# Out-gate of a decoder layer by seven block products, low weight parts by adding transfers, second values moved into the heads

## The chip, the cores and the metric

The kernel runs on one core of one Trainium2 chip. The metric is the device time of one execution in microseconds; for one core that is the time of that core. The time before is the median of three runs.

## The reference, cut to what matters

One layer works on 512 tokens and 1024 channels, in float32. Only what the change touches is shown.

```python
u = _rmsnorm(h, norm1_g[l])
proj = u @ w_in[l]
a_glu, q, k, v, r, g_low, gate_a, gate_b = _split_cols(proj)   # 2048|512|512|1024|1024|16|1024|1024

c = a_glu[..., :CONV_CH] * jax.nn.sigmoid(a_glu[..., CONV_CH:])
c = _causal_dwconv(c, conv_dw_w[l], conv_dw_b[l])               # 31 taps for each channel
c = jax.nn.silu(_layernorm(c, conv_ln_g[l], conv_ln_b[l]))      # over channels
y_conv = c @ w_conv_out[l]

gk = jax.nn.log_sigmoid((g_low @ w_gate_up[l] + b_gate[l]).astype(jnp.float32)) / GATE_NORMALIZER
o = _gla_chunked(qh, kh, vh, gkh)                               # 4 heads, dk 128, dv 256
o = o * lax.rsqrt(jnp.mean(o * o, axis=-1, keepdims=True) + EPS) * gla_norm_g[l]
o = o.reshape(bsz, seq, GLA_VDIM).astype(x.dtype) * jax.nn.silu(r)
y_gla = o @ w_gla_out[l]

merged = jax.nn.sigmoid(gate_a) * y_conv + jax.nn.sigmoid(gate_b) * y_gla
h = h + merged @ w_o[l]
# then a channel mixer (up-projection, 3-tap convolution, silu gate, down-projection) and a norm
```

The out-gate is `r`: a product of the 512 x 1024 activations `u` with a 1024 x 1024 slice of `w_in`, whose silu multiplies the normed output of the heads.

## The kernel before, in words

**Products in three parts.** Every large product is made from a high and a low part of both operands. A weight block of 128 x 1024 is loaded by a transfer on SP's queue (L174, tile `raw`, four buffers), ScalarE rounds it to the high part (L254, `whi`), VectorE subtracts to get the low part (L257, `wlo`; four buffers each). `mm3` (L299 to L301) issues three TensorE matmuls of 128 x 128 by 128 x 512 for each piece of a product. `col_tile` makes one 128-channel tile of the result for all 512 tokens: eight pieces, 24 matmuls, out of one weight block. `row_half` makes results that are token-major (128 tokens by 512 channels).

**Order of weights.** The list `order` holds all weight blocks in the order of their use: `w_v` (first half), `w_glu` (two blocks for each of eight channel tiles, the gate block first), `w_low`, `w_v` (second half), for each of the four heads `w_qk` twice and `w_r` twice, then `w_gb` and `w_gla` in turns, `w_ga`, `w_conv`, `w_o`, and the channel mixer's. `weight(name, j)` hands out the next block and, before that, splits the blocks up to `LOOK = 2` ahead (`prefetch`, `split_weight`); each split issues one more load (`load`), so that loads are four blocks ahead.

**Product by seven.** `w_o` and `w_down` are multiplied by a scheme with seven instead of eight block products (names `a11`, `a12`, `s1`, `n2`, `s4`, `n3`, `a22` in `STEPS`). The weight sums that it needs are made by transfers on the GpSimd queue that add onto a block that lies in SBUF (`sum_on`, L225, and `load_block`, L208) and by VectorE (`operand`); their blocks are split at L238 and L239.

**Work between.** The convolution's 240 VectorE steps (L591), the layer norm's sums (L614), centring (L639 to L646) and output (`ln_out`, L658 to L669) stand in lists, `chains`. `fill(RATE)`, called by every `weight`, takes pieces with shares that add up to 5 and traces them behind the last low part (`pace`). What the source traces is put in each engine's queue by a scheduler, by its own estimate of when an instruction can run; `manual_schedule` keeps the source's order for the first part (up to the end of the first values) and for one group of ScalarE's.

**The start.** The four token tiles are transposed (L374), tokens 0 and 1 are multiplied first without their norm factor (L467), tokens 2 and 3 are normed before they are transposed and split by `spread_gain` in pieces of 128 x 128 (L384, L386). `renormed` (L479) makes the normed `u` for tokens 0 and 1 after that. The result stands in `u1` as high and low parts; whole float32 values aren't kept.

**The heads.** In round `h` of the loop over heads the decays (L760, L762), queries and keys of head `h` are made, and scores, states and outputs of head `h - 1`; between these stand two tiles of the out-gate (`gate_r`, channel-major, silu at L860). `outputs` takes the root of the mean square by GpSimd (`rsqrt`, L347), ScalarE scales (L843); `gated` transposes (L849), VectorE multiplies with the gain and the gate's tile (L852), and the result is split (L668, L669). In a fifth round `w_gb` tiles stand in the gaps.

Of the kernel before, what the change touches and what calls it, by code (L numbers as in the profile page):

```python
# [36 lines left out]
RATE = 5.0  # L37
WARM = 10
# [3 lines left out]
SEVEN = {"w_o": KT // 2, "w_down": FT // 2}  # L42
# [6 lines left out]

C_A, C_G, C_Q, C_K, C_V, C_R = 0, 1024, 2048, 2560, 3072, 4096  # L50
# [15 lines left out]
def trunk_layer(ctx: ExitStack, tc: tile.TileContext, a: dict, out: bass.AP):  # L66
# [20 lines left out]
    gla_scope, gp = scoped("gla", 1, "right")  # L87

# [92 lines left out]
    def block(name, pairs, d, row, col):  # L181

        pairs = pairs[2 * d : 2 * d + 2]
        first = pairs[0][row]
        w = a[name][col * SEVEN[name] + first // 2]
        return w if len(pairs) == 2 else w[:, row * T : (row + 1) * T]

    def keep_tile(name):
        if name == "w_o":
            return tp.tile([P, D], F32, tag="x", name=nm("kept"), bufs=3)  # L190
        return fp.tile([P, D], F32, tag="kept", name=nm("kept"), bufs=2)
# [21 lines left out]
    def operand(raw, pairs, step, d):  # L213

        if step == "s4":
            return kept[pairs, d, "b22"]
        if step == "n2":
            nc.vector.tensor_tensor(kept[pairs, d], kept[pairs, d], raw, ALU.add)
        return raw if step in ("a12", "n3") else kept[pairs, d]

    def sum_on(name, pairs, step, d):

        if step in ("a11", "n2"):
            nxt = block(name, pairs, d, *((0, 1) if step == "a11" else (1, 0)))
            nc.gpsimd.dma_start(kept[pairs, d], nxt, accum_op=ALU.add)  # L225

    def split_weight(between=None):
        if len(ready) < len(order):
            while len(raws) <= len(ready):
                load()  # L230
            raw = raws[len(ready)]
            name, spec = order[len(ready)]
            if name in SEVEN:
                raw = operand(raw, *spec)
# [4 lines left out]
                nc.vector.tensor_tensor(lo, raw, hi.bitcast(F32), ALU.subtract)  # L239
                sum_on(name, *spec)  # L240
                ready.append((hi, lo))
                load()
                return
            hi = wp.tile([P, D], F32R, tag="whi", name=nm("whi"), bufs=4)
            if order[len(ready)][0] == "w_low":
                nc.scalar.copy(hi, raw)
                if order[len(ready)][1] == 0:
                    part_lo = lambda t: t.rearrange("p (k c) -> p k c", c=P)[:, :, :RANK]
                    nc.vector.tensor_tensor(part_lo(hi), part_lo(raw), part_lo(hi.bitcast(F32)), ALU.subtract)
                ready.append((hi, None))  # L250
                load()
                return
            lo = wp.tile([P, D], F32R, tag="wlo", name=nm("wlo"), bufs=4)
            nc.scalar.copy(hi, raw)  # L254
            if between:
                between()
            pace[0] = nc.vector.tensor_tensor(lo, raw, hi.bitcast(F32), ALU.subtract)  # L257
            ready.append((hi, lo))
            load()
# [6 lines left out]
    def weight(name, j, ahead=LOOK):  # L266
        assert order[used[0]] == (name, j)
        prefetch(1)
        used[0] += 1
        prefetch(ahead)  # L270
        fill(RATE)
        return ready[used[0] - 1]
# [199 lines left out]

    def renormed(t):
        rb = ax_bank()[:, :P]
        nc.tensor.matmul(rb, r1[t].to_broadcast([P, P]), ident, start=True, stop=True)
        rb = rb.unsqueeze(1).to_broadcast([P, 4, P])
        for g in range(2):
            f = unscaled[t, g]
            nc.vector.tensor_tensor(by_token(f), by_token(f), rb, ALU.mult)  # L479
        for g in range(2):  # L480
            f = unscaled[t, g]
            split_by(by_token(f), *(u1[g][i][:, :, t * P : (t + 1) * P] for i in range(2)))
# [45 lines left out]
    here = lambda t: (lambda g, k: tuple(u1[g][i][:, k, t * P : (t + 1) * P] for i in range(2)))  # L528
# [24 lines left out]
    spread_gain(banks[2], 0, here(2))  # L553
# [5 lines left out]
    spread_gain(banks[3], 0, here(3))  # L559
# [13 lines left out]
    def values(n, middle):  # L573
        row_half("w_v", n * KT // 2, n, acts1, KT, v_done, n == 1, middle)

# [4 lines left out]

    conv = [None] * KT

# [9 lines left out]

    for k in range(KT):
# [6 lines left out]
        chains.append(  # L600
            [(1 if tap < CW - 1 else 0, lambda k=k, tap=tap, c=c: conv_tap(k, tap, c)) for tap in reversed(range(CW))]
        )


    ca = [None] * KT
    stat = {}

    def add_up(tiles, key):
        def first():
            stat[key] = btmp()  # L610
            nc.vector.tensor_tensor(stat[key], tiles(0), tiles(1), ALU.add)

        def more(k):
            nc.vector.tensor_tensor(stat[key], stat[key], tiles(k), ALU.add)  # L614

        return [first] + [lambda k=k: more(k) for k in range(2, KT)]
# [55 lines left out]
    def norm_chain():  # L672
        chain = [(1, f) for f in add_up(lambda k: conv[k], "sum")]
        chain[-1] = (RATE, chain[-1][1])
        chain.append((0, ln_mean))
        chain.extend((2, lambda k=k: ln_center(k)) for k in range(KT))
        chain[-1] = (RATE, chain[-1][1])
        chain.append((RATE, ln_var))
# [29 lines left out]
    def gate(step):  # L708
        if step > 0:
            return  # L710
        with tc.manual_schedule(engines={ET.Activation}):
            for h in range(HEADS):
                pg = ax_bank() if h < 3 else mm_bank()
                nc.tensor.matmul(pg, gate_up[:, h * DK : (h + 1) * DK], glow, start=True, stop=True)
                bg = pp[:, PP_BG + h : PP_BG + h + 1]
                ab.append(heap())
                nc.scalar.activation(ab[h], pg, AF.Abs, bias=bg)
                ls.append(heap())
                nc.vector.tensor_scalar(ls[h], pg, bg, 0.0, ALU.add, ALU.min)
            for h in range(HEADS):  # L720
                nc.scalar.activation(ab[h], ab[h], AF.Exp, scale=-1.0)
            for h in range(HEADS):
                nc.scalar.activation(ab[h], ab[h], AF.Ln, bias=1.0)
                nc.vector.tensor_tensor(ls[h], ls[h], ab[h], ALU.subtract)

    values(1, gate)


# [17 lines left out]
    class Head:  # L746
# [77 lines left out]
        def outputs(self):  # L824
            self.o = tp.tile([P, NT, DV], F32, tag="x", name=nm("o"), bufs=3)
            for g in range(2):
# [14 lines left out]
                for i in range(2):  # L841
                    o = self.o[:, 2 * g + i, :]
                    nc.scalar.activation(o, po[:, i * DV : (i + 1) * DV], AF.Copy, scale=r[:, i : i + 1])  # L843

        def gated(self):
            for s in range(2):
# [3 lines left out]
                f = tmp()  # L850
                m = 2 * self.h + s
# [3 lines left out]
    sr = [None] * KT  # L855

    def gate_r(m):
        pr = col_tile(weight("w_r", m), acts1)
        sr[m] = heap()
        nc.scalar.activation(sr[m], pr, AF.Silu)  # L860

    gbs = {}

    def gate_b(m):
        gbs[m] = col_tile(weight("w_gb", m), acts1)


    heads = [Head(h) for h in range(HEADS)]
    for h in range(HEADS + 1):
# [5 lines left out]
        else:  # L875
            gate_b(0)
        if old:
            old.scores()
        new.keys() if new else gate_b(1)
        if old:  # L880
            old.states()
        gate_r(2 * h) if new else gate_b(2)
        if old:
            old.outputs()
        gate_r(2 * h + 1) if new else gate_b(3)
# [6 lines left out]
    part = [None] * KT  # L892
    ma = [None] * KT
    for m in range(KT):
        part[m] = heap()
        nc.scalar.activation(part[m], gbs.pop(m), AF.Sigmoid)
        py = col_tile(weight("w_gla", m), oa)
        if m + AHEAD < KT:
            gate_b(m + AHEAD)
        nc.vector.tensor_tensor(part[m], py, part[m], ALU.mult)  # L900
    gas = {}
    for m in range(KT):
        pg = col_tile(weight("w_ga", m), acts1)
        gas[m] = heap()
        nc.scalar.activation(gas[m], pg, AF.Sigmoid)
    while chains:
        fill(1)
    H = T // 2
# [362 lines left out]
```

## Time and profile before

| what | value |
|---|---|
| median of 3 runs | 840.23 us (839.93 to 840.76) |
| the profiled execution's own time | 841.55 us |
| its span (first to last instruction) | 839.8 us |
| granted TensorE clock | 0.998 |
| TensorE busy (PE) | 829.0 us, 99% |
| VectorE busy (DVE) | 650.0 us, 77% |
| ScalarE busy (ACT) | 397.6 us, 47% |
| GpSimd busy (POOL) | 45.0 us, 5% |

The page lists busy times of the engines, the span in 40 slices, the transfer queues (q1 is SP's, q0 is GpSimd's), the chain of work that ended last, the costliest groups of instructions by line with the mean duration of one in ns, and the transfers with the time to landing. A matmul's duration overlaps with the next one's; what a matmul costs is the distance of two starts. All times in the text are in microseconds from the start of the span.

### The profile page before, as it was taken

The numbers are of one execution on the slowest core, as the hardware profiler recorded it, in microseconds if no ns is written. First come the engines' busy times: TensorE is split into PE (matmuls) and PEld (weight loads), VectorE is DVE, ScalarE is ACT, GpSimd is POOL, SyncE is SP. The second block draws the span as 40 slices with busy tenths as digits, with TensorE's granted clock in tenths as the row PEclk, the third lists the DMA queues.
The fourth block names the chain that finished last, engine by engine and source line by source line (L and its number), as shares of the span: only waits on it lengthen the run. The fifth ranks groups of instructions, "written<-read, shape, count | busy, mean of one in ns | idle before, by whom it ended". The sixth has DMA issues, their size and how long they took to land.

```text
span 839.8 us, 10108 instructions
## 1 busy us (share of the span) xinstructions
PE 829.0 (99%) x3841; PEld 692.3 (82%) x3841; DVE 650.0 (77%) x953; ACT 397.6 (47%) x590; POOL 45.0 (5%) x64
## 2 busy tenths in 40 slices
PE   8999999999999999999999999999999999999996
PEld 7888888887888888888888898888888888888885
DVE  5689879999997799644678758778757787677795
ACT  5722337435443422449444766444434444444454
POOL 1000000002100100000001000000100010000111
PEclk9999999999999999999999999999999999999999
DMA  7332222222222322222347643234742249222452
GB/s 289 119 105 101 96 96 91 91 87 80 97 76 76 125 89 89 100 81 95 101 100 197 180 151 126 101 94 108 213 150 87 66 89 284 102 84 94 102 124 100
DMA packets 28609, 97.27 MB, mean 116 GB/s; under 512 B 3248, under 2 KB 3648, under 8 KB 28560
## 3 DMA queue, kind: packets, MB, share of 16 engines
q1 hardware_dynamic: 25072, 84.82, 28.9%
q0 software_dynamic: 3456, 11.80, 8.0%
q8 instruction: 30, 0.49, 0.2%
q14 instruction: 19, 0.16, 0.1%
q10 hardware_dynamic: 32, 0.01, 0.0%
HBM read 94.51 MB, written 2.10 MB: 115 GB/s over the span
## 4 chain that ended last, share of the span: by engine, by line
PE 87%; DVE 9%; ACT 1%; issue 1%; POOL 1%; POOLq 0%; ACTq 0%; DVEq 0%
PE mm L299 26%; PE mm L301 26%; PE mm L300 26%; DVE c L591 4%; DVE wlo L257 2%; PE ax L301 1%; PE ax L300 1%; PE ax L299 1%; POOL rstd L347 1%; PE ax L832 1%; PE ax L374 1%; PE ax L434 1%; PE ax L814 0%; PE ax L834 0%; PE ax L849 0%
## 5 line engine op out<-in xcount | busy, mean ns | idle before, releaser
L299 PE MATMUL mm<-uh,wlo 128*128 128x512 f32 (+1 forms) x768 | 295.1, 384 | 0.0
L301 PE MATMUL mm<-uh,whi 128*128 128x512 f32 (+1 forms) x768 | 292.6, 381 | 0.0
L300 PE MATMUL mm<-ul,whi 128*128 128x512 f32 (+1 forms) x768 | 292.4, 381 | 0.0
L254 ACT CAST whi<-raw 128x1024 fp32r<-128x1024 f32 x116 | 120.9, 1048 | 128.5 <-PE mm L301 97.0
L257 DVE TENSOR_TENSOR wlo<-raw,whi 128x1024 fp32r<-128x1024 f32 x116 | 141.3, 1221 | 34.5 <-ACT whi L254 34.3
L301 PEld LDWEIGHTS mm<-uh,whi 128*128 128x128 f32 x768 | 144.5, 188 | 27.7
L300 PEld LDWEIGHTS mm<-ul,whi 128*128 128x128 f32 x768 | 144.7, 188 | 27.1
L299 PEld LDWEIGHTS mm<-uh,wlo 128*128 128x128 f32 x768 | 144.6, 188 | 26.8
L591 DVE SCALAR_TENSOR_TENSOR c<-h,pp,c 128x511 f32<-128x511 f32 (+14 forms) x240 | 162.7, 734 | 0.7
L1054 DVE SCALAR_TENSOR_TENSOR tmp<-mm,pp,tmp 128x511 f32<-128x511 f32 x88 | 65.8, 749 | 66.7 <-ACT tmp L1052 65.6
L1052 ACT ACTIVATE tmp<-mm,pp 128x512 f32<-128x512 f32 x44 | 34.3, 779 | 61.6 <-PE mm L301 61.6
L238 ACT CAST whi<-kept 128x1024 fp32r<-128x1024 f32 (+1 forms) x32 | 31.6, 994 | 23.7 <-PE mm L301 10.4
L239 DVE TENSOR_TENSOR wlo<-kept,whi 128x1024 fp32r<-128x1024 f32 (+1 forms) x32 | 36.7, 1154 | 4.2 <-ACT whi L238 4.1
L997 DVE TENSOR_TENSOR hres<-hres,mm 128x512 f32<-128x512 f32 (+1 forms) x49 | 32.7, 672 | 6.0 <-PE mm L301 4.1
L238 ACT CAST whi<-raw 128x1024 fp32r<-128x1024 f32 (+1 forms) x24 | 23.7, 995 | 17.9 <-PE mm L301 17.7
L347 POOL TENSOR_TENSOR rstd<-var,mhalf 128x1 f32<-128x1 f32 (+1 forms) x16 | 16.6, 1046 | 239.3 <-DVE var L839 194.8
L239 DVE TENSOR_TENSOR wlo<-raw,whi 128x1024 fp32r<-128x1024 f32 (+1 forms) x24 | 27.4, 1154 | 2.2 <-ACT whi L238 2.1
L300 PE MATMUL mm<-wlo,sh 128*128 128x512 f32 x66 | 25.8, 391 | 0.0
L301 PE MATMUL mm<-whi,sh 128*128 128x512 f32 x66 | 25.7, 390 | 0.0
L299 PE MATMUL mm<-whi,sl 128*128 128x512 f32 x66 | 25.6, 390 | 0.0
L299 PE MATMUL mm<-h,wlo 128*128 128x512 f32 x64 | 25.4, 398 | 0.0
L225 POOL DMA_DIRECT2D kept<-in_w_down_dram x12 | 10.4, 863 | 272.9 <-DVE wlo L239 272.9
(253 smaller groups left out, 1165.6 us busy)
## 6 DMA issues: line engine op xcount, KB each, us to landing
raw<-in_w_up_dram SPq DMA_DIRECT2D x44, 512.0 KB, 3.4
raw<-in_w_glu_dram SPq DMA_DIRECT2D x16, 512.0 KB, 3.5
raw<-in_w_down_dram SPq DMA_DIRECT2D x15, 512.0 KB, 3.3
kept<-in_w_down_dram POOLq DMA_DIRECT2D x10, 512.0 KB, 5.2
raw<-in_w_v_dram SPq DMA_DIRECT2D x8, 512.0 KB, 4.1
raw<-in_w_qk_dram SPq DMA_DIRECT2D x8, 512.0 KB, 3.2
raw<-in_w_r_dram SPq DMA_DIRECT2D x8, 512.0 KB, 3.2
raw<-in_w_gb_dram SPq DMA_DIRECT2D x8, 512.0 KB, 3.3
```

Of the source, the lines that this page charges most:

```text
L238: nc.scalar.copy(hi, raw)
L239: nc.vector.tensor_tensor(lo, raw, hi.bitcast(F32), ALU.subtract)
L254: nc.scalar.copy(hi, raw)
L257: pace[0] = nc.vector.tensor_tensor(lo, raw, hi.bitcast(F32), ALU.subtract)
L299: nc.tensor.matmul(acc, ll, rh, start=first, stop=False, **kw)
L300: nc.tensor.matmul(acc, lh, rl, start=False, stop=False, **kw)
L301: nc.tensor.matmul(acc, lh, rh, start=False, stop=last, **kw)
L347: nc.gpsimd.tensor_tensor(r, v, mhalf[:, :n], ALU.pow)
L591: nc.vector.scalar_tensor_tensor(y[:, s:], c[:, : T - s], w, y[:, s:], ALU.mult, ALU.add)
L997: nc.vector.tensor_tensor(hres[t, n][:, c], hres[t, n][:, c], bank[of[step]][i][:, c], op)
L1052: nc.scalar.activation(z, acc, AF.Identity, bias=pp[:, PP_FB + m : PP_FB + m + 1], scale=w[2])
L1054: nc.vector.scalar_tensor_tensor(z[:, s:], acc[:, : T - s], w[j], z[:, s:], ALU.mult, ALU.add)
```

## The change

Five things change together.

1. **The out-gate by seven.** `w_r` joins `SEVEN`. A new routine `unit` makes seven block products, token-major, into six accumulators, right after `w_low` and before the heads: 7 products x 2 token tiles x 4 pieces x 3 matmuls. `r_sink` adds them up in eight tiles `sr[t, n]` and takes the silu. The weight sums come from adding transfers; one more than for `w_o` (the step from `s1` to `n2`). The activation sums `s1`, `n2`, `s4`, `n3` are formed by VectorE out of whole float32 values of `u`, which are now kept (`whole`); `sums_chain` puts the 16 pieces in `chains`. To have whole values, tokens 2 and 3 are multiplied with the gain and split as whole tiles (`gained_normed`) and no longer in pieces of 128 x 128.
2. **Rows in DRAM.** Eight calls of `lay_rows`, one for each channel tile of the convolution branch, copy `w_r` by two transfers each on SP's queue from its column blocks into eight row blocks `rows_r` in DRAM, in runs of 128 floats; the loads and additions of `w_r` read these.
3. **Low parts by adding transfers.** For the 31 blocks in `ADDED` (seven of `w_glu`, all eight of `w_qk`, `w_gb` and `w_gla`) ScalarE writes the negative high part into the low part's tile, and a transfer on GpSimd's queue adds the weight onto it. With the eight additions for `w_r` that makes 39 adding transfers.
4. **Late second values.** The second half of `w_v` moves into rounds 0 and 1 of the heads, where tiles of the out-gate stood, with four accumulators open at once; `w_gb` tiles take the gaps of rounds 2 to 4, and the first four `part` tiles are taken in round 4.
5. **Other order of small work.** `fill` gets a rate for each weight (`RATES`); the layer norm's sum is added up within the convolution's lists (`add_up`); the shares before and after its variance are 15. In `outputs` VectorE multiplies with the root and the gate; in `gated` ScalarE makes the high part and VectorE the low part right from the transposes. The decay gate's three groups stand in three places of `unit` (`GATE_AT`).

```diff
+RATES = {"w_glu": 6.2, "w_r": 0.3, "w_low": 0.0, "w_v": 5.5, "w_qk": 5.0, "w_gb": 6.0, "w_gla": 6.0, "w_ga": 9.0}
+ADDED = {("w_glu", 2 * k) for k in range(1, KT)} | {("w_qk", m) for m in range(KT)}
+ADDED |= {(name, m) for name in ("w_gb", "w_gla") for m in range(KT)}
+SEVEN = {"w_o": KT // 2, "w_down": FT // 2, "w_r": KT // 2}
+GATE_AT = [("a11", 1), ("a12", 0), ("n2", 1)]
...
+    dp = pool("rows", 1, bass.MemoryType.DRAM)
+    rows_r = [dp.tile([P, D], F32, name=f"rows{j}") for j in range(KT)]
+    def lay_rows(j):
+        n, k = j // 4, j % 4 * 2
+        for i in range(2):
+            src = a["w_r"][n * 4 : n * 4 + 4, :, (k + i) * P : (k + i + 1) * P]
+            dst = rows_r[j][:, i * T : (i + 1) * T]
+            nc.sync.dma_start(dst.rearrange("p (c x) -> p c x", x=P), src.rearrange("c p x -> p c x"))
...
-    order += [("w_v", KT // 2 + j) for j in range(KT // 2)]
+    order += [("w_r", (O_PAIRS, step, d)) for step, d in STEPS]
     for h in range(HEADS):
-        order += [("w_qk", 2 * h), ("w_qk", 2 * h + 1), ("w_r", 2 * h), ("w_r", 2 * h + 1)]
-    order += [("w_gb", m) for m in range(AHEAD)]
-    for m in range(KT):
-        order += [("w_gla", m)] + [("w_gb", m + AHEAD)] * (m + AHEAD < KT)
+        late_v = [("w_v", KT // 2 + 2 * h + j) for j in range(2)]
+        late_b = [("w_gb", 2 * (h - 2) + j) for j in range(2)]
+        q, k = ("w_qk", 2 * h), ("w_qk", 2 * h + 1)
+        order += [q, late_v[0], k, late_v[1]] if h == 0 else [q, k] + (late_v if h == 1 else late_b)
+    order += [("w_gb", m) for m in range(4, KT)]
+    order += [("w_gla", m) for m in range(KT)]
...
-        if step in ("a11", "n2"):
-            nxt = block(name, pairs, d, *((0, 1) if step == "a11" else (1, 0)))
+        where = {"a11": (0, 1), "n2": (1, 0)}
+        if name == "w_r":
+            where["s1"] = (1, 1)
+        if step in where:
+            nxt = block(name, pairs, d, *where[step])
             nc.gpsimd.dma_start(kept[pairs, d], nxt, accum_op=ALU.add)
...
             nc.scalar.copy(hi, raw)
+            if order[len(ready)] in ADDED:
+                nc.scalar.activation(lo, raw, AF.Copy, scale=-1.0)
+                nc.gpsimd.dma_start(lo, a[name][spec], accum_op=ALU.add)
+                ready.append((hi, lo))
+                load()
+                return
...
+    def gained_normed(t):
+        for g in range(2):
+            gain = gains[:, g * 4 : g * 4 + 4].unsqueeze(2).to_broadcast([P, 4, P])
+            nc.vector.tensor_tensor(into_whole(t, g)[0], by_token(banks[t][g]), gain, ALU.mult)
+        for g in range(2):
+            f, parts = into_whole(t, g)
+            split_by(f, *parts)
...
-    spread_gain(banks[2], 0, here(2))
+    gained_normed(2)
...
     for k in range(KT):
+        lay_rows(k)
         pg = col_tile(weight("w_glu", 2 * k + 1), acts1)
...
+    def unit(name, acts, sink, at=lambda step, i: None):
+        ...
+            for i in range(2):
+                if (of[step], i) not in bank:
+                    bank[of[step], i] = ax_bank() if step == "a12" else mm_bank()
+                acc = bank[of[step], i]
+                for d, w in parts:
+                    for j in range(2):
+                        ah, al = (x[:, i * P : (i + 1) * P] for x in acts(step, 2 * d + j))
+                        c = slice(j * T, (j + 1) * T)
+                        last = d == 1 and j == 1
+                        mm3(acc, (ah, al), (w[0][:, c], w[1][:, c]), opens and d == 0 and j == 0, last, not opens)
+                if parts[-1][0] == 1:
+                    at(step, i)
+                    sink(step, i, acc)
...
+    unit("w_r", quadrant, r_sink, r_at)
...
-                    nc.scalar.activation(o, po[:, i * DV : (i + 1) * DV], AF.Copy, scale=r[:, i : i + 1])
+                    gate = sr[t, self.h // 2][:, (self.h % 2) * DV : (self.h % 2 + 1) * DV]
+                    nc.vector.scalar_tensor_tensor(self.o[:, t, :], half, r[:, i : i + 1], gate, ALU.mult, ALU.mult)
...
-                nc.vector.scalar_tensor_tensor(f, po, pp[:, PP_GG + s : PP_GG + s + 1], sr[m], ALU.mult, ALU.mult)
-                oa[m] = split(f)
+                nc.scalar.activation(hi, po, AF.Copy, scale=gain)
+                nc.vector.scalar_tensor_tensor(lo, po, gain, hi.bitcast(F32), ALU.mult, ALU.subtract)
...
-        if old:
+            between(h, 0)
             old.outputs()
-        gate_r(2 * h + 1) if new else gate_b(3)
+        between(h, 1)
```

More of the change, by code (lines that the diff above doesn't have):

```diff
@@ L270, in weight @@
         prefetch(ahead)
-        fill(RATE)
+        fill(RATES.get(name, RATE))
         return ready[used[0] - 1]
@@ L526, in v_done @@
             nc.scalar.activation(vt[t, n], acc, AF.Copy, scale=r)
-    here = lambda t: (lambda g, k: tuple(u1[g][i][:, k, t * P : (t + 1) * P] for i in range(2)))
+    for half in range(2):
+        for g in range(2):
+            whole[half, g] = sum_tile()
     banks[0] = turned(xs[0])
@@ L601, in trunk_layer @@
             [(1 if tap < CW - 1 else 0, lambda k=k, tap=tap, c=c: conv_tap(k, tap, c)) for tap in reversed(range(CW))]
+            + [(1 if k else 0, lambda k=k: add_up(k))]
         )
     ca = [None] * KT
[L606 to L616, printed above, removed]
     def token_sums(s):
@@ L706, in trunk_layer, with gate @@
     ls, ab = [], []
-    def gate(step):
-        if step > 0:
-            return
+    def gate(piece):
         with tc.manual_schedule(engines={ET.Activation}):
             for h in range(HEADS):
[L713 to L724, printed above, removed]
```

183 lines of the change are left out of this document (144 added, 39 removed).

## The prediction

> **What bounds the kernel now.** I read the page's busy times, its slices and its chain first.
>
> ```profile
> span 839.8 us, 10108 instructions
> PE 829.0 (99%) x3841; PEld 692.3 (82%) x3841; DVE 650.0 (77%) x953; ACT 397.6 (47%) x590; POOL 45.0 (5%) x64
> PE   8999999999999999999999999999999999999996
> PE 87%; DVE 9%; ACT 1%; issue 1%; POOL 1%; POOLq 0%; ACTq 0%; DVEq 0%
> ```
>
> TensorE is busy in every slice but the first and the last. A busy PE need not be one at its pace, so next come the waits of PE (engine, line, waited for: total, times, longest) and the timeline of PE where the `w_glu` tiles begin (start, duration, engine, line).
>
> ```profile
> PE ax L434 <- DVE ones L403: 1.1, 1, 1.1
> PE ax L849 <- ACT o L843: 1.1, 1, 1.1
> PE mm L299 <- DVE hres L997: 0.5, 1, 0.5
> ...
> 34.57 0.39 PE L301 MATMUL mm<-whi,uh 128*128 128x512 f32 x1
> 34.80 0.39 PE L299 MATMUL mm<-uh,wlo 128*128 128x512 f32 x1
> 35.02 0.39 PE L300 MATMUL mm<-ul,whi 128*128 128x512 f32 x1
> 35.25 0.39 PE L301 MATMUL mm<-uh,whi 128*128 128x512 f32 x1
> 35.48 0.39 PE L299 MATMUL mm<-uh,wlo 128*128 128x512 f32 x1
> ```
>
> The three longest waits are 1.1, 1.1 and 0.5 us: there is next to nothing to win by taking waits away. Matmuls start 0.227 us apart (35.48 - 34.80, by three), also where token-major matmuls (34.57) turn into channel-major ones (34.80). So time is the number of matmuls by 0.227 us, and a change wins by issuing fewer, and loses where PE comes to wait.
>
> The Trainium skill (TensorE: Matmul & The Clock Gate, "Wait — 56ns, not 53.3ns?") gives 215.7 ns between starts of warm matmuls of 512 columns; the trace has 227 at full granted clock, and the measurement decides. By the page's figure the first term below would be 5.18 instead of 5.45 us.
>
> **Part 1, the matmuls.** The out-gate took 8 tiles of 24 matmuls, 192; it will take 7 x 2 x 4 x 3 = 168. Minus 24 by 0.227 us: **-5.45 us**. The second values, `w_gb` and all others keep their number.
>
> **Part 2, the start.** Tokens 2 and 3 are split in whole tiles. The timeline and the groups (count, then busy us and mean ns) show what this replaces:
>
> ```profile
> 20.51 2.15 ACT L384 ACTIVATE uh<-ax,gains 128x128 fp32r<-128x128 f32 x8
> 21.66 2.16 DVE L386 SCALAR_TENSOR_TENSOR ul<-ax,gains,uh 128x128 fp32r<-128x128 f32 x8 [0.32 <-ACT uh L384]
> 25.09 2.16 DVE L386 SCALAR_TENSOR_TENSOR ul<-ax,gains,uh 128x128 fp32r<-128x128 f32 x8 [0.87 <-ACT uh L384]
> ...
> L467 DVE TENSOR_TENSOR h<-ax,gains 128x512 f32<-128x512 f32 x3 | 2.1, 688 | 0.9 <-PE ax L374 0.9
> L458 ACT CAST uh<-h 128x512 fp32r<-128x512 f32 x4 | 2.4, 622 | 2.0 <-DVE h L479 2.0
> L459 DVE TENSOR_TENSOR ul<-h,uh 128x512 fp32r<-128x512 f32 x4 | 2.6, 688 | 0.2
> ```
>
> Before, the first low piece of token tile 3 is there at 25.09 + 0.34 = 25.4 and its matmuls begin about 26.2. After, VectorE multiplies twice (0.69 each), ScalarE copies (0.62), VectorE subtracts (0.69): the first low part comes 2.0 to 2.1 us after the start of the first multiplication, not 0.35 after that of the first subtraction. The order is kept by hand here; token tile 2's copies end about 0.7 us later than now, so ScalarE's squares for the next norm factor, and VectorE's sum behind them, are later by that too. I get 27.2 for tile 3's first low part against 26.2 and 0.2 for tile 2's. Bounds: 0 (if the scheduling of this part has that slack) and 1.5. I take the worked-out **+1.0 us**.
>
> **Part 3, the adding transfers.** A block in `ADDED` loses VectorE's 1.22 us and gains a second ScalarE pass and a transfer.
>
> ```profile
> L254 ACT CAST whi<-raw 128x1024 fp32r<-128x1024 f32 x116 | 120.9, 1048 | 128.5 <-PE mm L301 97.0
> L257 DVE TENSOR_TENSOR wlo<-raw,whi 128x1024 fp32r<-128x1024 f32 x116 | 141.3, 1221 | 34.5 <-ACT whi L254 34.3
> 40.93 1.04 ACT L254 CAST whi<-raw 128x1024 fp32r<-128x1024 f32 x1
> ...
> kept<-in_w_o_dram POOLq DMA_DIRECT2D x4, 512.0 KB, 6.1
> raw<-in_w_glu_dram SPq DMA_DIRECT2D x16, 512.0 KB, 3.5
> pp<-in_pp_dram SPq DMA_DIRECT2D x1, 227.0 KB, 9.2
> ...
> q1 hardware_dynamic: 25072, 84.82, 28.9%
> q0 software_dynamic: 3456, 11.80, 8.0%
> ```
>
> The cast at 40.93 is for the fifth `w_glu` block, whose tile starts at 34.80 + 4 x 24 x 0.227 = 56.6: it is released by a freed buffer, nearly three tiles ahead. The path is 1.05 + 1.05 on ScalarE and 6.1 to land, 8.2 of 15.7 us. So **0** on PE; it would need a landing time above 13 us to cost anything. VectorE is spared 31 x 1.22 = 38 us and pays some 6 for the seven's low parts, 11 for 16 pieces of sums, 6 for the out-gate's additions and nothing net in the heads: about 15 us less load. ScalarE pays 31 x 1.05 = 33 us, in stages where it is busy less than half of the time (the window rows of part 5). Transfers: 39 x 0.52 = 20.5 MB of adding ones at q0's price (8.0% of 839.8 for 11.8 MB, 5.7 us of all 16 engines per MB) is 117 us spread over the 250 us from `w_glu` to `w_gla`. It fits. GpSimd's queue now holds the roots of the heads and these additions, each of which waits for ScalarE; a root behind a late addition delays that head's output. Its price is the L849 row: 1.1 us each time.
>
> **Part 4, the seven's chain.** `s1` to `n2` goes by another addition. The second block of `s1` can't be split before the second block of `a11` frees its buffers, 24 matmuls or 5.45 us after `unit` begins. From there: cast 1.0, subtraction 1.15, landing 6.1, cast 1.0, subtraction 1.15 makes 15.9. It is used at 5.45 + 4 x 2.72 + 1.36 = 17.7. A margin of 1.8 us, in which ScalarE also has the decay gate's four exponentials and silus with table loads of 1.28 between them (row below). Bounds 0 and 2.5: I take **+0.6 us**.
>
> **Part 5, the heads.** One wait of 1.1 us (L849) may go; new are `outputs` through VectorE, which has a convolution piece in hand most of the time, and only one free accumulator in rounds 0 and 1, so that keys wait for the queries to be read. The window rows of two stages (interval, its length, busy us of PE, PEld, DVE, ACT and POOL with their instructions, clock, transfer share, GB/s):
>
> ```profile
> 34.80:122.00 87.20, 87.20 (x386) 72.31 (x385) 71.40 (x99) 28.37 (x34) 0.53 (x1) 1.00 0.34 116
> 148.00:289.00 141.00, 139.90 (x676) 117.83 (x675) 130.01 (x209) 62.33 (x109) 11.32 (x8) 1.00 0.26 90
> ...
> L591 DVE SCALAR_TENSOR_TENSOR c<-h,pp,c 128x511 f32<-128x511 f32 (+14 forms) x240 | 162.7, 734 | 0.7
> ```
>
> VectorE is busy 130 of 141 us in the heads, and only 1.1 us of PE's time is lost there. An instruction of the chain finds up to a piece of 0.7 us ahead of it; the matmul tile of 5.45 us between it and its reader covers several. Bounds -1.1 and +3; I take **+0.3 us**.
>
> **Part 6, the norm's tail.** Adding up the shares by `fill`'s rules, the spread of the norm's root goes in front of the sixth `w_ga` tile; before it is in front of the fourth.
>
> ```profile
> 372.38 0.89 PE ax L628 x8
> ...
> 399.94 0.61 ACT L668 CAST ch<-btmp 128x512 fp32r<-128x512 f32 x1
> L660 ACT ACTIVATE btmp<-c,pp 128x512 f32<-128x512 f32 x8 | 6.2, 811 | 0.3 <-DVE c L669 0.2
> L668 ACT CAST ch<-btmp 128x512 fp32r<-128x512 f32 x8 | 4.6, 610 | 0.0
> L660 ACT ACT_TABLE_LOAD x4 | 5.1, 1283 | 0.2
> L905 ACT ACT_TABLE_LOAD x4 | 5.1, 1283 | 0.1
> ```
>
> Now 28.2 us pass from the spread to the last `ch` (399.94 + 0.61 - 372.38); then there are 0.9 + 3 x 5.45 to the first `w_conv` tile and 4.8 more until its last piece is read, 22. ScalarE's own work in the 28 is 6.5 + 4.9 for the eight pieces, 10.2 for eight table loads between silu and sigmoid, and casts. The pieces will come five and three at a time, so I expect fewer loads. Bounds 0 and +6; I take **+0.7 us**.
>
> **Sum.** -5.45 + 1.0 + 0 + 0.6 + 0.3 + 0.7 = -2.85. The profiled execution took 841.55 (span 839.8 and 1.75 around it): it would be 838.7. The runs' median is 1.3 lower, 840.23: forecast **837.4 us**. By the page's pitch it would be 837.7.
>
> **Rivals.** *A, the copies in DRAM come first (slower).* The sixteen transfers of `lay_rows` depend on nothing, and the schedule moves such loads far ahead: in the SP timeline the two first `w_o` loads stand before a `w_gb` load that the list has some twenty blocks earlier.
>
> ```profile
> 5.65 0.33 SPq L133 DMA_DIRECT2D pp<-in_pp_dram  x1
> 10.88 9.12 SPq L174 DMA_DIRECT2D raw<-in_w_glu_dram  x4
> ...
> 282.27 0.90 SPq L206 DMA_DIRECT2D kept<-in_w_o_dram  x2
> 291.05 0.33 SPq L174 DMA_DIRECT2D raw<-in_w_gb_dram  x1
> ```
>
> They may then sit behind the load at 5.65 and ahead of the first `w_glu` load at 10.88. The load at 5.65 took 9.2 us to land though small, as it stood behind the loads of `x` and `w_v`: the queue was full until 14.9. The copies are 4.19 MB in 512-byte runs; no row shows a transfer within DRAM. At q1's price (28.9% of 839.8 for 84.82 MB, 2.86 us per MB) they take 12.0 us, at q0's (each byte moved twice) 23.9. The first `w_glu` block would land 1.5 us after (0.52 MB), at 28.4 or 40.3, and is ready for PE, two passes later, at 30.7 or 42.6, against 35.8 with the later start: nothing, or +6.8. It decides from 17 us of copying on, and turns the sum's sign from 20 on. At the upper end the time is 844.2. For it: the empty SP queue from 6 to 10.9. Against: the lower end is a plain price and fits, and the time needed is between the ends. The Trainium skill (DMA: Bandwidth & Descriptors, "Queues, rings and completion order") has it that an engine takes a queue's descriptors in ring order; the 9.2 us of the small load agree. By that rule alone the copies can't be overtaken, and the price is the one just given.
>
> *B, all cover holds.* If part 2's slack is there, parts 4 and 6 cost nothing and the wait at L849 goes: -5.45 - 1.1 + 0.3, 834.0.
>
> *C, ScalarE in the norm's tail is the bound.* If table loads stay eight, 28.2 against 22 puts +6 in place of 0.7: 842.7; with half of it 839.7, no change that could be told. For it: the eight loads alone are 10.2 of the 28 us. Against: the first `w_conv` tile reads the pieces one by one, and the last has 4.8 us more.
>
> *D, the seven don't spare matmuls' time.* If PE waits for `n2` and again for each sum, the 24 saved are lost as waits: 840.2 to 842. Against: `w_o` and `w_down` run the same scheme now, with waits of 0.5 us.
>
> **How the numbers follow.** Forecast 0.47 (835.5 to 839), B 0.12, A at over 4 us 0.19, C 0.12, D 0.06, others 0.04. The likeliest one's time is 837.4. Leaving out the tails of A and D and half of B, the range is 834.3 to 844.3. Faster means by over 0.2% (1.7 us, under 838.5), about what a measurement of this kernel can tell: 0.47 x 0.9 + 0.12 and a little of A with a short copy, 0.58. Within 0.2%: a part of C, D and the forecast, 0.13. Slower: 0.29.
>
> **What would show it.** 168 matmuls with `w_r`, starts 0.227 apart; a PE gap near 26 us of about 1; no PE wait for low parts written by a transfer; waits under 1 us in `unit` at `n2`; the spread at about the sixth `w_ga` tile and no gap above 2 us at the first `w_conv` tile. A is seen in the SP timeline (L-lines of `lay_rows` at 6 to 12 us) and a gap before the first `w_glu` matmul. The prediction is wrong if PE's waits add up to more than 5.5 us, or if its pace changes.

## The result, and the profile after

The changed kernel takes 845.44 us (median of 4 runs, 845.20 to 846.13) against 840.08 us (839.09 to 840.76) for the kernel before beside it: a ratio of 1.0066, 95% interval 1.0049 to 1.0084. It is slower by two thirds of a per cent. The forecast was 837.4 us, and the range ended at 844.3. The profiled execution took 845.25 us with a span of 843.5; before's profiled execution, at 841.55, lay above its own median, so the two traces differ by 3.7 us where the medians differ by 5.4. The working below explains the 3.7.

The page of the changed kernel, the same rows as were shown of before:

```profile
span 843.5 us, 10197 instructions
PE 826.5 (98%) x3817; PEld 687.2 (81%) x3817; DVE 637.2 (76%) x950; ACT 424.8 (50%) x608; POOL 76.0 (9%) x103
PE   8999999989999999999999999999999999999996
PE 83%; DMA 5%; DVE 4%; ACT 3%; issue 3%; POOL 1%; SPq 0%; POOLq 0%; ACTq 0%; DVEq 0%
...
q0 software_dynamic: 9072, 32.25, 22.5%
```

There are 24 matmuls fewer (3817 against 3841) and PE is busy for less time; still the span is longer. The chain of what ended last tells where to look: PE's share has gone from 87% to 83%, and transfers, which had none, hold 5%. The slices name a place too: one 8 among the nines, the ninth slice, which is 169 to 190 us. PE's waits (engine, line, waited for: total, times, longest) give the names.

```profile
PE mm L322 <- DMA wlo<-in_w_qk_dram: 3.6, 1, 3.6
PE mm L323 <- DVE wlo L256: 2.1, 3, 0.8
PE mm L322 <- DVE hres L1145: 1.3, 2, 0.8
```

Two things are new at the top. The first is one wait for a low part that an adding transfer writes: the keys' block of head 0. The timeline of PE shows its true price.

```profile
180.14 0.39 PE L324 MATMUL mm<-whi,uh 128*128 128x512 f32 x1
184.13 0.77 PE L322 MATMUL mm<-uh,wlo 128*128 128x512 f32 x1 [3.60 <-DMA wlo<-in_w_qk_dram]
184.69 0.63 PE L323 MATMUL mm<-ul,whi 128*128 128x512 f32 x1
185.12 0.63 PE L324 MATMUL mm<-uh,whi 128*128 128x512 f32 x1
...
187.17 0.40 PE L323 MATMUL mm<-ul,whi 128*128 128x512 f32 x1
```

Starts lie 3.99 us apart where 0.227 is the pace: 3.8 us lost. After that, matmuls start 0.43 us apart, and the eighth comes at 187.17, 3.04 us after the first; at the pace it would be 1.59. So another 1.5 us are lost after the wait has ended. The windows say why (interval, its length, busy us of PE, PEld, DVE, ACT, POOL, then granted clock, transfer share, GB/s):

```profile
125.80:169.50 43.70, 41.06 (x174) 31.91 (x173) 30.28 (x38) 36.20 (x47) 6.30 (x8) 1.00 0.78 177
180.00:184.00 4.00, 0.53 (x3) 0.10 (x1) 4.00 (x7) 1.99 (x2) 0.88 (x1) 0.96 1.00 255
184.00:187.00 3.00, 2.87 (x7) 2.33 (x8) 2.77 (x5) 0.00 (x0) 0.00 (x0) 0.50 1.04 276
187.00:190.00 3.00, 3.00 (x15) 2.44 (x14) 0.00 (x0) 0.00 (x0) 0.00 (x0) 0.99 1.06 274
```

The granted clock was 0.50 for three microseconds behind the idle one, and PE still counts as busy there. The Trainium skill (TensorE: Matmul & The Clock Gate, "What's actually happening") says that the clock is halved after an idle window of about 3.4 us and comes back after a busy one of the same length; the 4.0 us without a start agree; the 3.0 us at 0.50 behind them are a little shorter than that window, and the kernel without copies, below, has the clock halved after two shorter gaps.

Why was the low part late? ScalarE's timeline shows the beginning of its path, and GpSimd's the issue of the transfer. ScalarE's:

```profile
166.89 1.28 ACT L902 ACT_TABLE_LOAD   x1
168.19 0.63 ACT L902 ACTIVATE tmp<-b 128x512 f32<-128x512 f32 x1
168.84 1.28 ACT L837 ACT_TABLE_LOAD   x1
170.13 1.09 ACT L837 ACTIVATE h<-mm 128x512 f32<-128x512 f32 x2
171.24 1.28 ACT L903 ACT_TABLE_LOAD   x1
...
173.59 1.04 ACT L271 CAST whi<-raw 128x1024 fp32r<-128x1024 f32 x1
174.53 1.06 ACT L273 ACTIVATE wlo<-raw 128x1024 fp32r<-128x1024 f32 x1
```

And GpSimd's:

```profile
175.99 0.86 POOL L274 DMA_DIRECT2D wlo<-in_w_qk_dram  x1 [11.35 <-ACT wlo L273]
```

The block takes over buffers of `unit`'s last step, whose last matmul starts at 169.26; the cast ran at 173.59, behind an exponential, the silu of `a22`'s two tiles and another exponential, with a table load ahead of each change of function. The transfer was issued at 175.99 and landed about 8 us later.

The second new thing is the stretch of `unit`, 125.8 to 169.5: 43.7 us, where 168 matmuls and the gate's four small ones at 0.227 would be 39.0. PE's larger gaps there are at `n2`, `s4`, `n3` and `a22`, 3.7 us in five places; the first three:

```profile
144.51 0.39 PE L324 MATMUL mm<-whi,sum 128*128 128x512 f32 x1
145.30 0.50 PE L322 MATMUL mm<-whi,sum 128*128 128x512 f32 x1 [0.40 <-ACT whi L255]
146.56 0.50 PE L323 MATMUL mm<-wlo,sum 128*128 128x512 f32 x1 [0.76 <-DVE wlo L256]
...
150.68 0.51 PE L322 MATMUL mm<-whi,f 128*128 128x512 f32 x1
151.94 0.51 PE L323 MATMUL mm<-wlo,f 128*128 128x512 f32 x1 [0.76 <-DVE wlo L256]
```

They begin at the new addition, from `s1` to `n2`. GpSimd's timeline has its issue:

```profile
133.15 0.85 POOL L222 DMA_DIRECT2D raw<-rows  x1 [1.73 <-DMA raw<-rows]
134.64 0.89 POOL L242 DMA_DIRECT2D kept<-rows  x1 [0.64 <-DVE wlo L256]
```

ScalarE's timeline has what waited for it:

```profile
138.47 0.68 ACT L784 ACTIVATE h<-mm,pp 128x512 f32<-128x512 f32 x1
144.20 1.05 ACT L255 CAST whi<-kept 128x1024 fp32r<-128x1024 f32 x1 [5.05 <-DMA kept<-rows]
...
149.57 2.00 ACT L255 CAST whi<-raw 128x1024 fp32r<-128x1024 f32 x2
...
152.07 1.28 ACT L790 ACT_TABLE_LOAD   x1
153.36 2.20 ACT L790 ACTIVATE h<-h 128x512 f32<-128x512 f32 x4
...
155.93 2.00 ACT L255 CAST whi<-raw 128x1024 fp32r<-128x1024 f32 x2
```

The addition went out at 134.64 (the one at 133.15 is for `n3`) and landed about 9.5 us later. ScalarE takes its work in order, so it stood from 139.1 to 144.2 with the gate's functions, the copies out of the accumulators and the casts of `s4` and `n3` queued behind `n2`'s cast. Those of `s4` and `n3` then came late for PE.

### The profile page after: what moved, and what is told of

The parts are those of the page before. It is cut to its first block, busy times and chain, and to the rows that moved or that the text cites. A ratio compares the mean times of both kernels' runs of the same rounds, so it can differ in the third digit from the quotient of the medians.

```text
span 843.5 us, 10197 instructions
## 1 busy us (share of the span) xinstructions
PE 826.5 (98%) x3817; PEld 687.2 (81%) x3817; DVE 637.2 (76%) x950; ACT 424.8 (50%) x608; POOL 76.0 (9%) x103
## 4 chain that ended last, share of the span: by engine, by line
PE 83%; DMA 5%; DVE 4%; ACT 3%; issue 3%; POOL 1%; SPq 0%; POOLq 0%; ACTq 0%; DVEq 0%
PE mm L322 26%; PE mm L323 25%; PE mm L324 25%; DMA kept<-rows 1%; DMA kept<-in_w_down_dram 1%; DVE wlo L256 1%; DMA wlo<-in_w_qk_dram 1%; ACT whi L255 1%; DVE hres L1145 1%; PE ax L972 1%; DMA x<-in_x_dram 1%; DMA raw<-in_w_glu_dram 1%; PE ax L322 1%; PE ax L324 1%; PE ax L323 1%
## 5 line engine op out<-in xcount | busy, mean ns | idle before, releaser
L322 PE MATMUL mm<-uh,wlo 128*128 128x512 f32 (+1 forms) x704 | 270.4, 384 | 3.6 <-DMA wlo<-in_w_qk_dram 3.6
L324 PE MATMUL mm<-uh,whi 128*128 128x512 f32 (+1 forms) x704 | 267.8, 380 | 0.0
L323 PE MATMUL mm<-ul,whi 128*128 128x512 f32 (+1 forms) x704 | 267.6, 380 | 0.0
L664 DVE SCALAR_TENSOR_TENSOR c<-h,pp,c 128x507 f32<-128x507 f32 (+21 forms) x240 | 162.4, 731 | 1.2 <-ACT c L661 0.6
L322 PEld LDWEIGHTS mm<-uh,wlo 128*128 128x128 f32 x704 | 132.8, 189 | 28.9 <-DVE c L664 4.0
L324 PEld LDWEIGHTS mm<-uh,whi 128*128 128x128 f32 x704 | 132.7, 188 | 25.4
L323 PEld LDWEIGHTS mm<-ul,whi 128*128 128x128 f32 x704 | 132.9, 189 | 24.9 <-issue 0.2
L280 DVE TENSOR_TENSOR wlo<-raw,whi 128x1024 fp32r<-128x1024 f32 x77 | 93.4, 1219 | 14.8 <-ACT whi L271 14.6
L273 ACT ACTIVATE wlo<-raw 128x1024 fp32r<-128x1024 f32 x31 | 32.9, 1060 | 83.0 <-PE mm L322 77.1
L1145 DVE TENSOR_TENSOR hres<-hres,mm 128x512 f32<-128x512 f32 (+1 forms) x49 | 32.6, 671 | 3.9 <-PE mm L324 3.5
L322 PE MATMUL mm<-whi,ul 128*128 128x512 f32 x64 | 25.7, 402 | 0.3 <-DVE ul L482 0.2
```

What stands on the lines that cost most here:

```text
L273: nc.scalar.activation(lo, raw, AF.Copy, scale=-1.0)
L322: nc.tensor.matmul(acc, ll, rh, start=first, stop=False, **kw)
L323: nc.tensor.matmul(acc, lh, rl, start=False, stop=False, **kw)
L324: nc.tensor.matmul(acc, lh, rh, start=False, stop=last, **kw)
L664: nc.vector.scalar_tensor_tensor(y[:, s:], c[:, : T - s], w, y[:, s:], ALU.mult, ALU.add)
L1145: nc.vector.tensor_tensor(hres[t, n][:, c], hres[t, n][:, c], bank[of[step]][i][:, c], op)
```

## The experiments

The theory: the time over before is two separate losses, the keys' late low part with the slow clock behind it (5.3 us) and the waits in `unit` that begin at the new addition (3.7 us or more). Its rivals: the losses belong to the adding transfers' load as a whole, or to the copies in DRAM.

**The keys' second block split by VectorE.** One of the 39 is undone.

```diff
+ADDED -= {("w_qk", 1)}
```

> The changed kernel with one block less in ADDED: the second w_qk block (the keys of head 0) gets its low part from VectorE again. Theory: its adding transfer is the one that PE waits 3.6 us for at 180 us, and the slower clock behind that wait costs about 1.6 us more; both go, so 845.4 - 5.3 = 840.1. Rival (the adding transfers are late as a whole): the wait moves to the next added block and less than 1.5 us is won, 844 or more.

It took 838.92 us against 840.92 for before beside it (23 runs, 839.41 to 845.59), ratio 0.9974 (0.9960 to 0.9988). The span, 837.3, is 6.2 shorter than the changed kernel's: 5.3 by the wait and its clock, 0.8 by a wait at L1145 in the channel mixer that the changed kernel had twice and this one once. Of PE's waits the one for the transfer is gone and `unit`'s stay:

```profile
PE mm L324 <- DVE wlo L257: 2.2, 3, 0.8
```

**`n2` by VectorE**, the way `w_o` has it, with the rest of the change kept:

```diff
-        if step == "n2" and name != "w_r":
+        if step == "n2":
...
-        if name == "w_r":
-            where["s1"] = (1, 1)
```

> The changed kernel with the out-gate's n2 sum made by VectorE, as for w_o, and without the third addition in its chain. Theory: inside the seven products PE loses about 4.6 us, of which the waits at n2 (0.6 and 1.0) come from the second addition landing 9.5 us after its issue, with ScalarE standing still for 5.0 us; n2's go and part of s4's 1.0 behind them: 845.4 - 2 = 843.4 (842.8 to 844). Rival (ScalarE's order, with the decay gate's groups and their table loads between the casts, is the cause): under 0.7 us is won, since the casts still queue behind the same ScalarE work.

It took 838.13 us, ratio 0.9969 (0.9958 to 0.9980), 5 us better than expected. `unit`'s waits are gone, as the theory has it; but the theory kept the keys' wait whole, and that shrank as well. PE's waits:

```profile
PE mm L320 <- DVE c L662: 1.5, 1, 1.5
PE mm L320 <- DMA wlo<-in_w_qk_dram: 1.4, 1, 1.4
```

The windows right behind the two gaps:

```profile
168.00:171.00 3.00, 3.00 (x15) 2.46 (x14) 1.23 (x1) 3.00 (x5) 0.00 (x0) 1.00 0.01 4
180.00:183.00 3.00, 3.00 (x15) 2.47 (x14) 3.00 (x6) 0.00 (x0) 0.00 (x0) 1.00 1.09 220
```

Two gaps of 1.8 us between starts are left, at the two `w_qk` blocks of head 0, and behind them the granted clock stays at 1.00. The row that names the transfer is the queries' block, used at 166.53; the row that names `c` is the keys', used at 179.18. In the changed kernel the queries' block came just in time: its addition was issued at 163.76, took 5.5 us to land, and the first matmul with it started at 169.49. Here it was issued at 159.58, took 6.9 us, and PE waited. That wait moved the keys' turn back by as much, so of 3.8 us lost in one piece about 3.2 are left in two, and neither piece cost the clock. An earlier ScalarE isn't the reason: the keys' cast starts 3.9 us after the last matmul of `unit` is through (168.81 against 164.94), where it was 4.1 us (173.59 against 169.49). Why the queries' addition took longer here is not shown.

**No adding transfers for low parts.**

```diff
+ADDED = set()
```

> The changed kernel with ADDED empty: all low parts by VectorE, the seven and all else unchanged. Theory: the same 5.3 us as with the one block are won, and VectorE's 38 us more cost little since it has about 20% to spare outside the heads: 840 to 841.5. Rival (VectorE becomes the bound in w_glu and the heads, which is what the adding transfers were there for): low parts come late and it is 846 or slower.

It took 841.07 us, ratio 1.0000 (0.9989 to 1.0011). The keys' wait is gone, `unit`'s remain (L257 in its numbering), and a wait appears that adding transfers had hidden: PE stands 1.3 us for VectorE at the norm's mean. PE's waits:

```profile
PE mm L324 <- DVE wlo L257: 2.1, 3, 0.8
PE ax L707 <- DVE btmp L672: 1.3, 1, 1.3
```

**Rows without copies.** No `lay_rows`; the kernel gets `w_r` in rows already, as it gets `w_o`.

```diff
...
-        lay_rows(k)
...
-        "w_r": _cols(w_in, tiles(C_R, KT)),
+        "w_r": _rows(w_in, (C_R, C_R + T)),
```

> The changed kernel without the copies in DRAM: the host lays w_r out in rows, the sixteen transfers fall away. Theory: the copies ran from 14 to 32 us beside the w_glu loads and cost PE at most the 0.5 us by which a load of x came later, so 844.9 (844.5 to 845.4). Rival A of the prediction (the copies hold up the first weights): 4 us or more are won, 841.4 or less.

It took 845.93 us, ratio 1.0061 (1.0047 to 1.0075), with the same span as the changed kernel, 843.5. So the time shows no cost of the copies, and the rival that put the whole loss on them falls. Inside, the two traces differ. Without the copies the first `w_glu` matmul started at 34.23 instead of 35.15. In `unit` more was lost: two gaps of 1.4 and 1.3 us, with one matmul between them, ended at 144.96 and 146.22, and from 147.6 to 150.6 the granted clock was 0.50 and matmuls started 0.43 us apart. The wait for the keys was 4.2 us. Whether the copies cost the 0.9 us at the start, one trace can't tell.

**Both repairs, and both `w_qk` blocks of head 0.** The edits of the first two together; then, on top, the queries' block by VectorE too (`ADDED -= {("w_qk", 0), ("w_qk", 1)}`).

> The changed kernel with both repairs: n2 by VectorE, and the second w_qk block's low part by VectorE. Theory (two separate places): n2's repair alone left one wait of 1.6 us on the second w_qk block and one of 1.6 us before the first; the former goes: 838.1 - 1.6 = 836.5. Rival (both repairs act on one cause, ScalarE's lateness after unit): nothing beyond the first, 838.

> n2 by VectorE, and neither of head 0's w_qk blocks in ADDED. Theory: both waits behind unit were low parts that land late, so 838.1 - 3.2 = 834.9; PE is then left with the start's waits alone. Rival (the wait of 1.6 us before the first w_qk tile is for an accumulator or for VectorE, as the profile's row names it): no better than with the second block alone, 836.5.

They took 836.14 us, ratio 0.9944 (0.9932 to 0.9956), and 835.72 us, 0.9945 (0.9933 to 0.9957). The first came out as its theory had it. The second lies between its theory (834.9) and its rival (836.5) and decides neither, since the first left only 0.5 us of wait at the queries' block. Of the second's PE waits none lies in `unit` or in the heads:

```profile
PE ax L456 <- DVE ones L425: 1.1, 1, 1.1
...
PE mm L321 <- DVE hres L1144: 0.5, 1, 0.5
```

This also corrects a name, and the rival of the second, which has that row at the queries' block. The row that has PE waiting for a convolution step (`c`, L662) stood at the keys' block, and it is gone in both kernels, where VectorE makes that block's low part. PE had waited for the transfer and not for that step. These two are the best kernels of the study and beat both given ones; between them no difference can be told.

**The seven repaired, and nothing added.** `n2` by VectorE and `ADDED` empty.

> n2 by VectorE and ADDED empty: the seven products without any low part by a transfer. Theory: with ADDED empty and the third addition in place it was 841.1 with 4.6 us of waits in unit; these go: 837 (836 to 838), VectorE's lateness at the layer norm's mean (1.7 us) stays. So the matmuls' 5.45 us are had without the adding transfers, which are worth 1 to 2 us at most. Rival (the adding transfers are what makes room for the seven): 840 or more.

It took 837.51 us, ratio 0.9964 (0.9951 to 0.9977). So 3.4 of the 5.45 us that the seven spare show as time without any adding transfer for low parts (837.51 against 840.86 for before beside it). Those bring some more where they don't wait: 837.51 against 835.72, 1.8 us, as VectorE is again late for the norm's mean (1.3) and once in `unit` (`h`, L785, 1.0).

**The 31 adding transfers alone, in the kernel before.**

```diff
...
+            if order[len(ready)] in ADDED:
+                nc.scalar.activation(lo, raw, AF.Copy, scale=-1.0)
+                nc.gpsimd.dma_start(lo, a[name][spec], accum_op=ALU.add)
+                ready.append((hi, lo))
+                load()
+                return
```

> The kernel before with nothing but the adding transfers for the 31 blocks in ADDED (rates, order and the eight-block out-gate as before). Theory: away from the seven products a low part has some 15 us from its buffer to its use and needs about 9, so nothing changes: 840.9 (840 to 841.9), with VectorE's busy time down by about 38 us. Rival (adding transfers land late under load): PE waits for low parts in the heads, 843 or more.

It took 846.45 us (six runs, 844.08 to 848.19), ratio 1.0066 (1.0050 to 1.0082): as much slower as the whole change, and not the 840.9 expected. The theory had the loss at one block of the change's own order; here another order makes another block late. PE's waits:

```profile
PE mm L307 <- DMA wlo<-in_w_qk_dram: 3.8, 1, 3.8
```

PE's timeline:

```profile
147.59 0.39 PE L309 MATMUL mm<-whi,uh 128*128 128x512 f32 x1
151.73 0.50 PE L307 MATMUL mm<-uh,wlo 128*128 128x512 f32 x1 [3.75 <-DMA wlo<-in_w_qk_dram]
```

The windows from the gap on:

```profile
147.00:152.00 5.00, 1.25 (x6) 0.75 (x5) 5.00 (x7) 4.79 (x7) 0.00 (x0) 1.00 1.01 232
152.00:155.00 3.00, 3.00 (x9) 2.30 (x9) 3.00 (x9) 0.63 (x2) 0.00 (x0) 0.53 0.65 209
```

And ScalarE's timeline for that block:

```profile
130.81 1.05 ACT L256 CAST whi<-raw 128x1024 fp32r<-128x1024 f32 x1 [3.19 <-issue]
...
139.00 2.19 ACT L731 ACTIVATE h<-h 128x512 f32<-128x512 f32 x4
141.10 1.05 ACT L258 ACTIVATE wlo<-raw 128x1024 fp32r<-128x1024 f32 x1
```

The high part was there at 131.9, but the negative one ran only at 141.1, since the decay gate's group, whose order is kept by hand, came between the two passes with its two table loads (its last step, L731, is shown). The transfer then took 9 us to land, with all transfer engines busy (share 1.01). The mechanism is that of the changed kernel, at another block, the queries' of head 0: ScalarE late, the landing slow, the clock halved behind the idle time.

**Ahead of the keys' cast, two silus made copies** (they are left out in this kernel), which takes two table loads out of ScalarE's queue; the rest of the change is as it was.

```diff
-            nc.scalar.activation(sr[key], acc, AF.Silu)
+            nc.scalar.copy(sr[key], acc)
```

> The changed kernel with the silu of the last two out-gate tiles (a22) replaced by a copy, so that one table load before it and one behind it (1.28 us each) leave ScalarE's queue just ahead of the cast of the keys' second block. The computation lacks that silu. Theory (the wait of 3.6 us for the keys of head 0 is ScalarE's lateness plus a slow landing, and the slow clock follows from the long idle): the cast comes 2.6 us earlier, the wait shrinks to 1 to 1.5 us, matmuls no longer start 427 ns apart behind it, and the time falls by about 4.2 us to 841 (840.5 to 842). Rival (the landing is bound by the transfers that are in flight, and an earlier issue lands no earlier): the wait stays above 3 us, 844.5 to 845.5. The waits inside unit (about 4.6 us) stay in both.

It took 840.51 us, ratio 0.9995 (0.9985 to 1.0005), and the span is 839.7 where the changed kernel's is 843.5. The wait is 2.3 us shorter, nearly what the two table loads took (2.6), and no matmul behind it starts 427 ns after the last. PE's waits:

```profile
PE mm L323 <- DVE wlo L256: 2.2, 3, 0.8
PE mm L322 <- DMA wlo<-in_w_qk_dram: 1.3, 1, 1.3
```

So the lateness on ScalarE is a cause, and the rival falls: issued 3.0 us earlier (173.02 against 175.99), the transfer was there 2.4 us earlier (181.69 against 184.13), although it took 8.5 us to land where it had taken 8.0. And that lateness arises behind `unit`: the waits inside `unit` are as before. What a shorter landing would have given isn't tested.

**The 31 without the first `w_qk` block, in the kernel before.** One line more than in the kernel with all 31.

```diff
+ADDED -= {("w_qk", 0)}
```

> The kernel before with 30 adding transfers for low parts: all of the change's but the one for the first w_qk block, whose low part VectorE makes as before. Theory (of the 31, only the block whose path begins late on ScalarE, behind the decay gate's hand-kept group, makes PE wait; the slow clock follows from that one idle): the gap of 4.1 us at 147.6 and the matmuls 427 ns apart behind it go, and the time is 840 to 841.5, as the kernel before. Rival (any added block in this stretch is late, since the landing takes 8 to 9 us there): the wait moves to the second w_qk block or to the next one and 3 us or more stay, 843.5 to 846.

It took 840.75 us against 841.22, ratio 0.9997 (0.9988 to 1.0006), span 839.0 where it was 844.4 with all 31: 5.4 us back, and the wait moved to no other block. In this kernel thirty adding transfers cost nothing; one cost 5.4 us.

## Why the prediction was wrong, by its own steps

Two of its own signs of being wrong came: PE's waits add up to 10.5 us, against the 5.5 that it named, and the pace changed behind the keys' wait.

- **Part 1, the matmuls (-5.45): right.** 24 fewer were issued, 0.227 us apart, and from the first `w_glu` matmul to the last `w_conv` one the best kernel needs 403.0 us where before needs 408.8: 5.8 less, of which the wait at L849 gave 1.1, with some small new ones against it.
- **Part 2, the start (+1.0): too high.** The first `w_glu` matmul came at 35.15 against 34.80, +0.35. At tile 3 PE waited 0.2 us for the low part, where the prediction had about 1. How much of the 0.35 is the split by whole tiles and how much the copies isn't known (34.23 without copies).
- **Part 3, the adding transfers (0): this is the step that failed.** It measured 5.3 us at one block. The path was 8.2 us in the prediction and took 10.4: 2.4 from the cast's start to the issue and 8.0 to land. What failed above all was the lead. It was read from one cast in the `w_glu` stage, where each tile frees a buffer and a block has three tiles of time, 15.7 us, and it was taken for all 31. At the turn from `unit` to the heads the keys' block is used two tiles, 10.9 us, after `unit`, which would just have covered the path; but its cast began 4.1 us late, and PE lost 3.8. ScalarE was "busy less than half of the time" only on average, since the windows row above has it busy for 36.2 of 43.7 us in `unit`, with table loads right where the cast was due. The landing of 6.1 us was that of `w_o`'s additions; after, the DMA issues give a median of 7.3 for `w_qk`:

```profile
wlo<-in_w_qk_dram POOLq DMA_DIRECT2D x8, 512.0 KB, 7.3
wlo<-in_w_gb_dram POOLq DMA_DIRECT2D x8, 512.0 KB, 5.5
```

  Nothing in the prediction priced the granted clock: of the 5.3 us, 1.5 came when the wait was over. The other 30 did cost nothing, but for the queries' block of head 0 that was close: it had about 0.2 us to spare.
- **Part 4, the seven's chain (+0.6, bounds 0 and 2.5): the right place, the wrong size.** It measured 3.7 us in named gaps, 4.6 with the small ones. The chain was summed up with a margin of 1.8; the issue was 1.2 us later than its sum (134.64, against 125.82 + 5.45 + 2.15), of which 0.5 went by while VectorE ended a convolution step and 0.4 between the subtraction's end and the issue; and the landing was 3.4 longer than its 6.1. Less the margin, and less the 1.2 us by which PE itself came later to `n2`, that gives the 1.6 us of the first two gaps. The rest is ScalarE's order: the prediction counted the gate's work as a delay of the cast, not the cast as a delay of all that is queued behind it. Parts 3 and 4 also don't add: with part 4's waits gone, PE waited at the queries' block first, and the keys' wait became shorter and no longer cost the clock.
- **Part 5, the heads (+0.3): at its lower end, -1.1.** The wait at L849 went and none came. It went in the kernel before with 31 and with 30 adding transfers as well, so the new `outputs` isn't needed to explain it.
- **Part 6, the norm's tail (+0.7): 0.** Table loads fell from eight to six, and PE was busy for all of the 29.0 us of 375 to 404.
- **The rest:** +0.6 behind the last `w_conv` matmul, with 0.8 more of waits at L1145, which no part of the change touches; the changed kernel and the one with both repairs have that wait twice, the others of the study once. With -5.45 + 0.35 + 5.3 + 3.7 - 1.1 + 0.6 the sum is 3.4 of the 3.7 measured.
- **The rivals.** A named the right sign for the wrong reason. The copies did share SP's queue with `w_glu`'s loads, three of them ahead of the first, but no wait of PE names a `w_glu` block, and without copies the time was the same. D, the waits that eat up the seven's gain, is what `unit` did by two thirds; it was given 0.06 since `w_o` and `w_down` run the same scheme with waits of 0.5 us, but they make `n2` by VectorE, and with `n2` made so the waits went. C didn't happen. None of the rivals was a late low part from a transfer, although the prediction named what would show it: a PE wait for one.

What stays open: why the landing was 9.5 us at 134.64, 8 at 175.99 and 5.5 at 163.76 was not taken apart; the rows only show the first two beside a transfer share of 0.78 and 1.00. Halving that load alone was not tried.

## What to carry to other kernels

A lead that is read in one stage holds in that stage: before an operation is put on a longer path, find the block with the least time from its freed buffer to its use, and look at what its in-order engine has queued at that moment, table loads included. A wait in an in-order queue is paid by all that stands behind it. Where two operands in a row are late, the wait for the first gives the second time, so their prices don't add. When thirty of thirty-one uses are free, undo the one that waits and keep the rest.

## What the runs showed of the hardware that was not expected

- After 4.0 and 4.1 us without a matmul's start the granted clock was 0.50 and 0.53 for some 3 us and matmuls started 427 ns apart; after single gaps of 1.8 us it stayed at 1.00. It isn't one gap's length alone: in the kernel without copies two gaps of 1.4 and 1.3 us with one matmul between them were followed by 3 us at 0.50 too, which 0.8 and 1.3 us at the same place in the changed kernel were not. The wait of 3.8 us at the keys so cost 1.5 us more than itself.
- Adding transfers of 512 KB differ in their landing within one kernel: 5.5 us for the queries' block of head 0, 8.0 for the keys', 9.5 for the second `n2` sum, and in the median 5.5 for `w_gb` and 7.3 for `w_qk`.
- Sixteen transfers within DRAM, 4.19 MB in runs of 512 bytes, ran beside the loads of the start without a cost that the time shows (845.93 without them against 845.44; ratios to before 1.0061 and 1.0066).
